# The last feed-forward of a two-layer DiT block: the gate goes into the second weights, the last output slice is made in two halves

## The chip, the cores and the metric

One core of a Trainium2 chip runs the whole program. The metric is the device time of one execution in microseconds (us). Its engines are TensorE (PE, matrix products), VectorE (DVE), ScalarE (ACT), GpSimd (POOL, idle here) and SyncE (SP, which here only issues DMAs). Each engine works through its own queue in order, and waits on semaphores for the others.

## The reference, cut to what matters

The change lies in the last step of the last layer, the second feed-forward (SwiGLU with a gate, 22 blocks of 128 hidden channels), and in the final norm behind it:

```python
# last layer; x is (256 tokens, 1024); m = the layer's nine modulation vectors
h = modulate(rms_norm(x), m[6], m[7])
g, u = jnp.split(h @ w_gu, 2, axis=-1)            # w_gu (1024, 2 * 2816)
x = x + 0.5 * m[8] * ((silu(g) * u) @ w_down)     # w_down (2816, 1024)
return rms_norm(x) * final_gain
```

## The kernel before

All products are in 32-bit pieces: a weight block arrives as a raw 128x2048 tile (`raw`, three buffers), and each of its two halves (128x1024) is split by `Feeder.split` into a high part, which ACT casts (L189), and a low part, raw minus high, which DVE subtracts (L167). A product is then high*high + high*low + low*high. A raw tile is free for the next DMA when both halves are split. At most eight split halves are alive (`feed.limit = 8`).

Which instruction stands where in a queue is decided at build time: `Sched` keeps a clock of estimated PE time, `S.pe(ns)` advances it, and at each step `Feeder.tick` may emit the next split and waiting tasks may emit their next piece. On the chip the queues then run in that fixed order.

`ffn_last` works on pairs of hidden blocks, j = 0, 2, ... 20. For a pair PE makes four projections (g of both blocks, u of both blocks; L1416 and L1420, 24 matmuls each), each into one of four PSUM banks (`ps`) that the pairs reuse in turn. ACT copies one half of the bank (L1432) and DVE adds the other half (L1434), which frees the bank; for g, ACT then makes the silu (L1440); for u, DVE multiplies it in (L1445), ACT casts the result to its high part (L1447) and DVE subtracts the low part (L1450). After the projections of pair j, PE makes the second product (`down`, L1470 to L1472) for the two blocks of pair j - 2, into four other banks `acc[T, h]` (T: tokens 0 to 127 or 128 to 255, h: left or right 512 output columns). In a pair's stretch ACT and DVE therefore also split six halves: four of g and u, and two of the second weights (`f11d...`). The second weights of pair j stand in the plan behind g and u of pair j + 2; those of blocks 20 and 21 (`d10`) stand last.

The last pair's second products are made by `last_down` (L1590 to L1592), one slice (T, h) after the other: first blocks 18 and 19 (`early`), then 20 and 21 (`late`). `residual` then multiplies the slice by the gate (L1549, `grow` is the gate vector spread over all partitions), adds it to the tokens `xtok` (L1550) and ACT squares and sums it (L1553); `root`, `inverse` and `scaled` make the norm, and `store` writes the four slices out, three issued from SP and the last from ACT (L1572).

Ahead of all this, while the norm of x is computed, PE transposes the left half of x to token order (`turn(0, T)`, L1479) and spreads the gate (`spread`, L1487); the right half is transposed after the projections of pair 0 (`turn(1, T)`).

Of the kernel before, what the change touches and what calls it, by code (L numbers as in the profile page):

```python
# [126 lines left out]
class Feeder:  # L127


    def __init__(self, nc, pool, S, tile_):  # L130
        self.nc, self.pool, self.S, self.tile = nc, pool, S, tile_
        self.limit = 6
        self.max_block = 1
        self.next = 0.0
        self.hold = True
        self.lag = 0
        self.part = None
        self.t_dma = {}
        self.plan = []
        self.blocks = []  # L140
        self.index = {}
        self.raw = {}
        self.live = {}
        self.n_dma = self.n_split = 0
        self.raw_live = self.half_live = 0
# [29 lines left out]
    def split(self):  # L175
        self.flush()
        self.load()
        if self.n_split >= len(self.plan) or self.half_live >= self.limit:
            return False
        name, h = self.plan[self.n_split]  # L180
        if name not in self.raw:
            return False
        b = self.blocks[self.index[name]]
        src = b["halves"][h](self.raw[name])
        i = self.n_split
        view = (lambda t: t.rearrange("p (a b) -> p a b", a=src.shape[1])) if len(src.shape) == 3 else (lambda t: t[:, :])
# [68 lines left out]
def tile_hybrid_dit(  # L255
# [86 lines left out]
    def ffn_plan(l, w):  # L342
        gu = (f1_gu, f2_gu)[w][l].rearrange("(k p) c -> p k c", p=P)
        dn = (f1_dn, f2_dn)[w][l].rearrange("(f p) c -> p f c", p=P)
        key = f"f{l}{w}"

        def batch(a, b):
            for f in range(a, b, 2):
                feed.add_block(
                    f"{key}d{f // 2}", [(lambda t: k3(t, 2), dn[:, f:f + 2, :])], None,  # L350
                    [lambda t, h=h: t[:, h * 1024:(h + 1) * 1024] for h in range(2)],
                )
                feed.plan.extend([(f"{key}d{f // 2}", 0), (f"{key}d{f // 2}", 1)])

        alone = l == 1 and w == 1
        for j in range(NF):
            if j % 2 == 0:
                cols_block(f"{key}g{j // 2}", gu[:, :, j * P:(j + 2) * P])
                cols_block(f"{key}u{j // 2}", gu[:, :, DFF + j * P:DFF + (j + 2) * P])
                feed.plan.extend([(f"{key}{nm}{j // 2}", h) for nm in "gu" for h in range(2)])  # L360
                if alone and j:
                    batch(j - 2, j)
            if j in BATCH_AT and not alone:
                batch(*BATCH_AT[j])
        if alone:
            batch(20, 22)
            return
        batch(16, 18)
        batch(18, 22)
# [1037 lines left out]
    def ffn_last(h_task):  # L1407


        key = "f11"  # L1410
        grow, gain, xtok = a4(), a4(), [a4() for _ in range(2)]
        nc.scalar.dma_start(out=gain, in_=final_gain.rearrange("(o p) -> o p", o=1).partition_broadcast(P))
        acts = {}

# [60 lines left out]
        def turn(h, T, copy):  # L1475

            ps = psum()
            for q in range(4):
                nc.tensor.transpose(ps[:, q * P:(q + 1) * P], xT[:, 4 * h + q, T * P:(T + 1) * P], ident)  # L1479
            S.pe(4 * 117)  # L1480
            copy(xtok[T][:, h * 512:(h + 1) * 512], ps)

        def spread(h):

# [8 lines left out]
        wts = [feed.get(k) for k in kk[:3]]  # L1493
        need_ada(1, 8)
        for T in range(2):
            turn(0, T, nc.vector.tensor_copy)
        S.step(h_task)
        spread(0)()
        S.step(h_task)
        owed = spread(1)  # L1500
        wts.append(feed.get(kk[3]))
        S.finish(h_task)
        owed()
        feed.hold = False
        pss = [psum() for _ in kk]
        for k in range(KD):
# [4 lines left out]
        for k in kk:  # L1511
            feed.done(k)
        evict(0, pss)
        for T in range(2):
            turn(1, T, nc.scalar.copy)
        feed.limit = 8
        acc = {}
        order = [(T, h) for T in range(2) for h in range(2)]
# [22 lines left out]
        ss = st(4)  # L1541

        def residual(T, h, parts=1):
            t = t2()
            w = 512 // parts
            for i in range(parts):
                cs = slice(h * 512 + i * w, h * 512 + (i + 1) * w)
                tc_ = t[:, i * w:(i + 1) * w]
                nc.vector.tensor_mul(tc_, acc[T, h][:, i * w:(i + 1) * w], grow[:, cs])  # L1549
                nc.vector.tensor_add(xtok[T][:, cs], xtok[T][:, cs], tc_)  # L1550
            cs = slice(h * 512, (h + 1) * 512)
            i = 2 * T + h
            nc.scalar.activation(out=t2(), in_=xtok[T][:, cs], func=AF.Square, accum_out=ss[:, i:i + 1])  # L1553
            if h == 0:
                nc.scalar.activation(
                    out=ss[:, i:i + 1], in_=ss[:, i:i + 1], func=AF.Identity, bias=epsb[:, 0:1], scale=1.0 / D
                )

        def root(T):
            rms = st(1)  # L1560
            nc.scalar.activation(
                out=rms, in_=ss[:, 2 * T + 1:2 * T + 2], func=AF.Sqrt, bias=ss[:, 2 * T:2 * T + 1], scale=1.0 / D
            )
            return rms

# [3 lines left out]
            return rs  # L1569

        def store(T, h, o):
            (nc.scalar if T and h else nc.sync).dma_start(out=out[T * P:(T + 1) * P, h * 512:(h + 1) * 512], in_=o)  # L1572

        def scaled(T, h, rs):
            cs = slice(h * 512, (h + 1) * 512)
# [3 lines left out]
            )  # L1579
            store(T, h, o)  # L1580

        def last_down(T, h, fs):
            for f in fs:
                if f in act_tasks:
                    S.finish(act_tasks.pop(f))
                whi, wlo = feed.get((f"{key}d{f // 2}", f % 2))
                at = acts[f]
                cs, o = slice(h * 512, (h + 1) * 512), acc[T, h]
                ph, pl = at[:, T * P:(T + 1) * P], at[:, 256 + T * P:256 + (T + 1) * P]
                mm(o, ph, whi[:, cs], start=False, stop=False)  # L1590
                mm(o, pl, whi[:, cs], start=False, stop=False)
                mm(o, ph, wlo[:, cs], start=False, stop=(f == NF - 1))  # L1592
                S.pe(681)

        last_down(0, 0, early)
        last_down(0, 1, early)
        last_down(1, 0, early)
        last_down(0, 0, late)
        residual(0, 0)
        last_down(0, 1, late)  # L1600
        residual(0, 1)
        rms0 = root(0)
        last_down(1, 0, late)
        residual(1, 0)
        rs0 = inverse(rms0)
        scaled(0, 0, rs0)
        last_down(1, 1, early)
        last_down(1, 1, late)
        residual(1, 1, 2)
        xg = t2()  # L1610
        nc.vector.tensor_mul(xg, xtok[1][:, 512:1024], gain[:, 512:1024])
        scaled(0, 1, rs0)
        rs1 = inverse(root(1))
        o = t2()
        nc.scalar.activation(out=o, in_=xg, func=AF.Copy, scale=rs1[:, 0:1])
        scaled(1, 0, rs1)
# [34 lines left out]
```

## Time and profile before

| what | value |
|---|---|
| median of three runs | 1600.36 us (1599.35 to 1601.63) |
| the profiled execution | 1599.29 us, its span 1597.5 us |
| PE busy | 1575.7 us, 99% of the span |
| DVE busy | 1076.9 us, 67% |
| ACT busy | 601.4 us, 38% |
| the last feed-forward | its first projection starts at 1405.04 us, its last matmul at 1588.58 us |

The span is what the trace covers; the execution is 1.8 us longer. Times in rows of the trace are microseconds from the span's start. "Idle before" is the time that the engine stood still ahead of an instruction, with what released it.

### The profile page before, as it was taken

The page shows a single profiled execution, that of the slowest core. Times are in us where ns is not written, and L with a number is a line of the kernel's source. Part 1 is how long each engine was busy: PE and PEld are TensorE (multiplying, and loading weights), DVE is VectorE, ACT ScalarE, POOL GpSimd, SP SyncE. Part 2 cuts the span into 40 slices and gives each one's busy share as a digit, 9 for nine tenths or more (in the row PEclk, how much of TensorE's full clock was granted, in tenths as well). Part 3 has the DMA queues.
Part 4 walks back from the last instruction along what each step waited for, and adds up shares of the span by engine and source line. Part 5 has one row for each costly group of instructions (what it writes and reads, how often), then busy time and mean ns, then how long its engine had stood idle before and what let it go on. Part 6 is the DMA issues. An engine that isn't in the chain of part 4 may idle for free.

```text
span 1597.5 us, 20934 instructions
## 1 busy us (share of the span) xinstructions
PE 1575.7 (99%) x8455; PEld 1320.2 (83%) x8455; DVE 1076.9 (67%) x1672; ACT 601.4 (38%) x1007; POOL 0.8 (0%) x6
## 2 busy tenths in 40 slices
PE   7999999999999999999999999999999999999997
PEld 5888888888886998888888898888888898888886
DVE  4877878786856576765734576766566488776655
ACT  4423231133557452223231343222222356765553
POOL 0000000000000000000000000000000000000000
PEclk9999999999999999999999999999999999999999
DMA  9755565553012434534333315455564224346560
GB/s 333 271 182 198 163 205 200 171 196 106 33 54 54 132 110 164 172 132 158 121 103 106 123 60 184 165 195 184 187 215 165 93 99 101 112 159 223 185 211 27
DMA packets 149345, 241.71 MB, mean 151 GB/s; under 512 B 6484, under 2 KB 115712, under 8 KB 148992
## 3 DMA queue, kind: packets, MB, share of 16 engines
q1 hardware_dynamic: 147008, 238.71, 44.9%
q10 hardware_dynamic: 2240, 1.65, 0.3%
q8 instruction: 67, 1.10, 0.3%
q14 instruction: 30, 0.25, 0.1%
HBM read 239.29 MB, written 1.05 MB: 150 GB/s over the span
## 4 chain that ended last, share of the span: by engine, by line
PE 96%; DVE 2%; SPq 1%; DMA 1%; ACT 0%; issue 0%; ACTq 0%
PE ps L428 24%; PE ps L429 24%; PE ps L430 24%; PE ps L1416 5%; PE ps L1420 3%; PE ps L969 2%; PE ps L971 2%; PE ps L970 2%; PE ps L1190 1%; PE ps L1167 1%; PE ps L1470 1%; PE ps L1472 1%; PE ps L1471 1%; PE ps L654 1%; SPq L328 1%; DMA a<-in_ada_w_dram 1%
## 5 line engine op out<-in xcount | busy, mean ns | idle before, releaser
L428 PE MATMUL ps<-ahi,a 128*128 128x512 f32 (+1 forms) x1312 | 479.6, 366 | 1.2 <-ACT ahi L530 0.7
L429 PE MATMUL ps<-alo,a 128*128 128x512 f32 (+1 forms) x1312 | 477.5, 364 | 0.9 <-DVE alo L534 0.7
L430 PE MATMUL ps<-ahi,a 128*128 128x512 f32 (+1 forms) x1312 | 476.8, 363 | 0.0
L167 DVE TENSOR_TENSOR a<-raw,a 128x1024 fp32r<-128x1024 f32 x296 | 356.4, 1220 | 152.7 <-ACT a L189 152.7
L189 ACT CAST a<-raw 128x1024 fp32r<-128x1024 f32 x296 | 300.4, 1044 | 204.5 <-PE ps L429 78.1
L428 PEld LDWEIGHTS ps<-ahi,a 128*128 128x128 f32 x1312 | 247.4, 189 | 48.2 <-issue 6.0
L429 PEld LDWEIGHTS ps<-alo,a 128*128 128x128 f32 x1312 | 247.5, 189 | 40.4 <-DVE alo L534 1.8
L430 PEld LDWEIGHTS ps<-ahi,a 128*128 128x128 f32 x1312 | 247.4, 189 | 39.3 <-DVE a L212 0.2
L630 DVE SCALAR_TENSOR_TENSOR a<-ada,c,a 128x1024 f32<-128x1024 f32 x196 | 248.8, 1277 | 17.2 <-DMA ada<-in_ada_w_dram 17.1
L428 PE MATMUL ps<-a,a 128*128 128x512 f32 (+1 forms) x624 | 223.8, 359 | 0.0
L430 PE MATMUL ps<-a,a 128*128 128x512 f32 (+1 forms) x624 | 222.5, 357 | 0.0
L429 PE MATMUL ps<-a,a 128*128 128x512 f32 (+1 forms) x624 | 222.4, 356 | 0.0
L763 DVE SCALAR_TENSOR_TENSOR xT<-ps,modT,xT 128x256 f32<-128x256 f32 x288 | 126.5, 477 | 80.5 <-PE ps L430 80.3
L728 ACT CAST a<-t 128x512 fp32r<-128x512 f32 x66 | 41.0, 622 | 253.7 <-DVE t L726 253.7
L428 PEld LDWEIGHTS ps<-a,a 128*128 128x128 f32 x624 | 117.9, 189 | 20.8 <-issue 4.2
L430 PEld LDWEIGHTS ps<-a,a 128*128 128x128 f32 x624 | 117.9, 189 | 17.0
L429 PEld LDWEIGHTS ps<-a,a 128*128 128x128 f32 x624 | 117.9, 189 | 16.7
L721 ACT ACTIVATE t<-ps 128x512 f32<-128x512 f32 x66 | 39.3, 598 | 231.5 <-PE ps L430 225.1
L726 DVE TENSOR_TENSOR t<-ps,t 128x512 f32<-128x512 f32 x66 | 45.3, 690 | 82.1 <-PE ps L430 74.5
L1416 PE MATMUL ps<-ahi,a 128*128 128x512 f32 x352 | 90.5, 392 | 0.7 <-DVE ahi L534 0.7
L1416 PEld LDWEIGHTS ps<-ahi,a 128*128 128x128 f32 x352 | 63.6, 189 | 12.0 <-DVE ahi L534 0.9
L530 ACT ACTIVATE ahi<-t,modT 128x256 fp32r<-128x256 f32 x88 | 43.7, 508 | 54.6 <-DVE t L527 54.5
(176 smaller groups left out, 1378.1 us busy)
## 6 DMA issues: line engine op xcount, KB each, us to landing
raw<-in_ffn_w_gu_dram SPq DMA_DIRECT2D x88, 1024.0 KB, 5.2
ada<-in_ada_w_dram SPq DMA_DIRECT2D x128, 512.0 KB, 5.4
raw<-in_ffn_w_down_dram SPq DMA_DIRECT2D x44, 1024.0 KB, 4.9
raw<-in_w_in_dram SPq DMA_DIRECT2D x10, 1024.0 KB, 5.1
a<-in_ada_w_dram SPq DMA_DIRECT2D x16, 512.0 KB, 8.9
raw<-in_w_out_dram SPq DMA_DIRECT2D x16, 256.0 KB, 4.2
raw<-in_w_out_dram SPq DMA_DIRECT2D x8, 512.0 KB, 6.0
raw<-tab_pool SPq DMA_DIRECT2D x2, 1024.0 KB, 4.8
```

The costliest lines, as they stand in the source:

```text
L167: self.nc.vector.tensor_sub(vl, src, vh.bitcast(F32))
L189: self.nc.scalar.copy(vh, src)
L428: mm(ps, whi, mhi, start=start, stop=False)
L429: mm(ps, whi, mlo, start=False, stop=False)
L430: mm(ps, wlo, mhi, start=False, stop=stop)
L530: nc.scalar.activation(out=ahi[:, d, seg_cols(s)], in_=t, func=AF.Identity, bias=mod(l, m, d, s))
L630: nc.vector.scalar_tensor_tensor(out=acc, in0=raw, scalar=sc, in1=acc, op0=ALU.mult, op1=ALU.add,)
L726: nc.vector.tensor_mul(a[:, :n], u[:, :n], sg[:, :n])
L728: nc.scalar.copy(at[:, 0:n], a[:, :n])
L763: nc.vector.scalar_tensor_tensor(out=xs, in0=ps[:, q * 256:(q + 1) * 256], scalar=mod(l, m0 + 2, d, s), in1=xs, op0=ALU.mult, op1=ALU.add,)
L1416: mm(ps, wt[0][:, k, :], ahi[:, k, :], start=(k == 0), stop=(k == KD - 1))
L1420: mm(ps[:, 0:256], wt[1][:, k, :], ahi[:, k, 0:256], start=False, stop=False)
```

## The change

Three things change, all in the last feed-forward.

1. The gate is multiplied into the second weights. `Feeder.split` now multiplies a half of a `f11d` block by `grow`, in place, on DVE, ahead of ACT's cast of it; in return `residual` no longer multiplies the slice, and adds it straight from PSUM. There are 22 such halves.
2. The last slice (T = 1, right columns) of `last_down` with blocks 20 and 21 is made in two halves of 256 columns, each with its own residual and square, so there are five squares; `scaled(0, 1)` moves ahead of that, and all four stores are issued from SP.
3. `turn(1, T)`, which transposes the right half of x, moves into the norm's wait, ahead of the first projections; its two copies on ACT come right after the norm.

```diff
         src = b["halves"][h](self.raw[name])
+        if name in self.gated:
+            self.nc.vector.tensor_mul(src, src, self.gate)
...
         self.nc.scalar.copy(vh, src)
...
         if alone:
             batch(20, 22)
+            feed.gated.update(f"{key}d{f}" for f in range(NF // 2))
             return
...
+        feed.gate = grow
...
-        owed = spread(1)
+        owed = [spread(1)] + [turn(1, T, nc.scalar.copy) for T in range(2)]
         wts.append(feed.get(kk[3]))
         S.finish(h_task)
-        owed()
+        for late_copy in owed:
+            late_copy()
...
         evict(0, pss)
-        for T in range(2):
-            turn(1, T, nc.scalar.copy)
...
+        def residual(T, c0, c1, i):
+            h, a = divmod(c0, 512)
+            nc.vector.tensor_add(xtok[T][:, c0:c1], xtok[T][:, c0:c1], acc[T, h][:, a:a + c1 - c0])
+            square(T, c0, c1, i)
...
-            (nc.scalar if T and h else nc.sync).dma_start(out=out[T * P:(T + 1) * P, h * 512:(h + 1) * 512], in_=o)
+            nc.sync.dma_start(out=out[T * P:(T + 1) * P, h * 512:(h + 1) * 512], in_=o)
...
         scaled(0, 0, rs0)
-        last_down(1, 1, early)
-        last_down(1, 1, late)
-        residual(1, 1, 2)
+        last_down(1, early, 512, 1024)
+        scaled(0, 1, rs0)
+        last_down(1, late, 512, 768)
+        residual(1, 512, 768, 3)
+        last_down(1, late, 768, 1024)
+        residual(1, 768, 1024, 4)
+        rms1 = root(4)
         xg = t2()
         nc.vector.tensor_mul(xg, xtok[1][:, 512:1024], gain[:, 512:1024])
-        scaled(0, 1, rs0)
-        rs1 = inverse(root(1))
+        rs1 = inverse(rms1)
```

Lines of the kernel shift by a few: the add of a projection is L1434 before and L1440 in the change, the product L1445 and L1451, the low part of an activation L1450 and L1456, the low part of a weight L167 and L169; the new multiply is L188.

DVE's queue in one pair of the kernel before, from the third projection's add to the last split of the pair (`a` and `raw` are split and raw weights, `t` the activations, `ps` a projection's bank; what an instruction waits for stands in brackets):

```order
L1434 TENSOR_TENSOR t_2135_13059<-ps_13034,t_2134_13057 128x256 [waits DVE_49,Activation_49]
L1445 TENSOR_TENSOR t_2135_13059<-t_2135_13059,t_2124_13005 128x256 [waits DVE_49]
L1450 TENSOR_TENSOR t_2136_13062<-t_2135_13059,t_2136_13062 128x256 [waits Activation_49]
L167 TENSOR_TENSOR a_2139_13067<-raw_12957,a_2138_13066 128x1024 [waits DMAHW0_49,Activation_49]
L1434 TENSOR_TENSOR t_2141_13088<-ps_13064,t_2140_13086 128x256 [waits Activation_49]
L1445 TENSOR_TENSOR t_2141_13088<-t_2141_13088,t_2130_13032 128x256 [waits DVE_49]
L1450 TENSOR_TENSOR t_2142_13091<-t_2141_13088,t_2142_13091 128x256 [waits Activation_49]
L167 TENSOR_TENSOR a_2144_13097<-raw_12957,a_2143_13096 128x1024 [waits Activation_49]
```

The same place of DVE's queue in the changed kernel:

```order
L1440 TENSOR_TENSOR t_2135_13075<-ps_13050,t_2134_13073 128x256 [waits DVE_49,Activation_49]
L1451 TENSOR_TENSOR t_2135_13075<-t_2135_13075,t_2124_13021 128x256 [waits DVE_49]
L188 TENSOR_TENSOR raw_12973<-raw_12973,a_1867_11709 128x1024 [waits DMAHW0_49]
L1456 TENSOR_TENSOR t_2136_13078<-t_2135_13075,t_2136_13078 128x256 [waits Activation_49]
L169 TENSOR_TENSOR a_2139_13084<-raw_12973,a_2138_13083 128x1024 [waits Activation_49]
L1440 TENSOR_TENSOR t_2141_13105<-ps_13080,t_2140_13103 128x256 [waits Activation_49]
L1451 TENSOR_TENSOR t_2141_13105<-t_2141_13105,t_2130_13048 128x256 [waits DVE_49]
L188 TENSOR_TENSOR raw_12973<-raw_12973,a_1867_11709 128x1024
L1456 TENSOR_TENSOR t_2142_13108<-t_2141_13105,t_2142_13108 128x256 [waits Activation_49]
L169 TENSOR_TENSOR a_2144_13115<-raw_12973,a_2143_13114 128x1024 [waits Activation_49]
```

Each product is now followed by a multiply of a raw half by the gate (`a_1867`), and ACT's cast of that half, whose result the L169 two rows on takes, waits for it.

DVE's queue where the second weights of blocks 20 and 21 (`raw_13158`) are split, up to the product of block 20, in the changed kernel (in the kernel before the same rows stand there without the two L188):

```order
L169 TENSOR_TENSOR a_2172_13265<-raw_13125,a_2171_13264 128x1024 [waits Activation_49]
L188 TENSOR_TENSOR raw_13158<-raw_13158,a_1867_11709 128x1024 [waits DMAHW4_49]
L169 TENSOR_TENSOR a_2174_13283<-raw_13158,a_2173_13282 128x1024 [waits Activation_49]
L188 TENSOR_TENSOR raw_13158<-raw_13158,a_1867_11709 128x1024
L169 TENSOR_TENSOR a_2177_13299<-raw_13158,a_2176_13298 128x1024 [waits PE_49,Activation_49]
L1440 TENSOR_TENSOR t_2179_13319<-ps_13295,t_2178_13317 128x256 [waits Activation_49]
L1440 TENSOR_TENSOR t_2183_13342<-ps_13323,t_2182_13340 128x256 [waits Activation_49]
L1440 TENSOR_TENSOR t_2187_13365<-ps_13346,t_2186_13363 128x256 [waits DVE_49,Activation_49]
L1451 TENSOR_TENSOR t_2187_13365<-t_2187_13365,t_2180_13321 128x256 [waits DVE_49]
```

All adds of the last pair's projections (L1440) stand behind both multiplies and both subtractions of the last weight block, and so do, on ACT, their copies behind its casts.

PE's queue at the last slice, blocks 20 and 21, in the kernel before (`ps_12042` is `acc[1, 1]`):

```order
L1590 MATMUL ps_12042<-a_2173_13261,t_2188_13346 128x512
L1591 MATMUL ps_12042<-a_2173_13261,t_2188_13346 128x512
L1592 MATMUL ps_12042<-a_2174_13262,t_2188_13346 128x512
L1590 MATMUL ps_12042<-a_2176_13276,t_2192_13371 128x512
L1591 MATMUL ps_12042<-a_2176_13276,t_2192_13371 128x512
L1592 MATMUL ps_12042<-a_2177_13277,t_2192_13371 128x512
```

The same place of PE's queue in the changed kernel (`a_2173` to `a_2177` are the split second weights, `ps_12045` is `acc[1, 1]`):

```order
L1596 MATMUL ps_12045<-a_2173_13282,t_2188_13368 128x256
L1597 MATMUL ps_12045<-a_2173_13282,t_2188_13368 128x256
L1598 MATMUL ps_12045<-a_2174_13283,t_2188_13368 128x256
L1596 MATMUL ps_12045<-a_2176_13298,t_2192_13393 128x256
L1597 MATMUL ps_12045<-a_2176_13298,t_2192_13393 128x256
L1598 MATMUL ps_12045<-a_2177_13299,t_2192_13393 128x256
L1596 MATMUL ps_12045<-a_2173_13282,t_2188_13368 128x256 [waits DVE_49]
L1597 MATMUL ps_12045<-a_2173_13282,t_2188_13368 128x256
L1598 MATMUL ps_12045<-a_2174_13283,t_2188_13368 128x256
L1596 MATMUL ps_12045<-a_2176_13298,t_2192_13393 128x256
```

Six matmuls of 512 columns became twelve of 256, and the seventh waits for DVE: for the add that reads the first half out of the same bank.

## Rows read from the trace of the kernel before

**Rows 1.** The waits of PE, 1395 to 1600 us: us in total, times, longest

```profile
PE ps L1416 <- DVE ahi L534: 0.7, 1, 0.7
```

**Rows 2.** Timeline of DVE, 1441.5 to 1457 us: start, length, instruction

```profile
1441.75 0.42 DVE L1434 TENSOR_TENSOR t<-ps,t 128x256 f32<-128x256 f32 x1
...
1451.15 0.42 DVE L1434 TENSOR_TENSOR t<-ps,t 128x256 f32<-128x256 f32 x1
1451.60 0.42 DVE L1445 TENSOR_TENSOR t<-t,t 128x256 f32<-128x256 f32 x1
...
1453.45 3.50 DVE L167 TENSOR_TENSOR a<-raw,a 128x1024 fp32r<-128x1024 f32 x3 [0.53 <-ACT a L189]
1456.87 0.42 DVE L1434 TENSOR_TENSOR t<-ps,t 128x256 f32<-128x256 f32 x1
```

**Rows 3.** Timeline of ACT, 1441 to 1457 us

```profile
1442.20 0.42 ACT L1440 ACTIVATE t<-t 128x256 f32<-128x256 f32 x1 [1.74 <-DVE t L1434]
...
1452.06 0.41 ACT L1447 CAST t<-t 128x256 fp32r<-128x256 f32 x1 [1.81 <-DVE t L1445]
1452.37 2.94 ACT L189 CAST a<-raw 128x1024 fp32r<-128x1024 f32 x3
1455.22 0.36 ACT L1432 COPY t<-ps 128x256 f32<-128x256 f32 x1
```

**Rows 4.** Timeline of PE: a projection's end, two in a row, the first last_down

```profile
1428.15 0.40 PE L1416 MATMUL ps<-ahi,a 128*128 128x512 f32 x1
...
1572.09 2.00 PE L1416 MATMUL ps<-ahi,a 128*128 128x512 f32 x8
...
1574.88 0.40 PE L1416 MATMUL ps<-ahi,a 128*128 128x512 f32 x1
...
1577.91 0.40 PE L1590 MATMUL ps<-a,t 128*128 128x512 f32 x1
```

**Rows 5.** Groups by line, DVE, 1400 to 1600 us: busy, mean ns, idle before

```profile
L167 DVE TENSOR_TENSOR a<-raw,a 128x1024 fp32r<-128x1024 f32 x62 | 74.1, 1222 | 35.6 <-ACT a L189 35.6
```

**Rows 6.** Timeline of ACT: the copy of pair 2's fourth projection

```profile
1434.76 0.36 ACT L1432 COPY t<-ps 128x256 f32<-128x256 f32 x1
```

**Rows 7.** Timeline: low part of block 21's activation, and its first use on PE

```profile
1579.92 0.43 DVE L1450 TENSOR_TENSOR t<-t,t 128x256 fp32r<-128x256 f32 x1 [0.47 <-ACT t L1447]
...
1582.91 0.39 PE L1591 MATMUL ps<-a,t 128*128 128x512 f32 x1
```

**Rows 8.** Timeline of PE at the first projection and at the right half's transposes

```profile
1405.04 0.50 PE L1416 MATMUL ps<-ahi,a 128*128 128x512 f32 x1 [0.74 <-DVE ahi L534]
...
1416.34 1.03 PE L1479 MATMUL ps<-small,xT 128*128 128x128 f32 x8
1417.13 0.47 PE L1416 MATMUL ps<-ahi,a 128*128 128x512 f32 x1
```

**Rows 9.** Timeline of the end, 1588 to 1594 us

```profile
1588.58 0.39 PE L1592 MATMUL ps<-a,t 128*128 128x512 f32 x1
...
1590.72 0.63 ACT L1553 ACTIVATE t<-a 128x512 f32<-128x512 f32 x1 [1.93 <-DVE a L1550]
...
1591.99 0.16 DVE L1568 RECIPROCAL st<-st 128x1 f32<-128x1 f32 x1
...
1592.24 0.72 ACT L1615 ACTIVATE t<-t,st 128x512 f32<-128x512 f32 x1 [0.47 <-DVE st L1568]
1593.00 0.37 ACTq L1572 DMA_DIRECT2D out_dram<-t  x1
```

**Rows 10.** DMA issues, 1587 to 1598 us: count, KB each, us to landing

```profile
out_dram<-t SPq DMA_DIRECT2D x3, 256.0 KB, 2.0
out_dram<-t ACTq DMA_DIRECT2D x1, 256.0 KB, 3.7
```

**Rows 11.** A stretch behind the last matmul: us, engines' busy time, PEclk, DMA

```profile
1594.00:1595.00 1.00, 0.00 (x0) 0.00 (x0) 0.00 (x0) 0.00 (x0) 0.00 (x0) 0.50 1.00 373
```

**Rows 12.** Timeline of PE: the first transposes of the program

```profile
6.04 3.68 PE L465 MATMUL ps<-small,a 128*128 128x128 f32 x16 [0.94 <-DMA a<-in_x_dram]
```

More of the change, by code (lines that the diff above doesn't have):

```diff
@@ L138, in __init__ @@
         self.t_dma = {}
+        self.gated = set()
+        self.gate = None
         self.plan = []
@@ L1480, in turn @@
             S.pe(4 * 117)
-            copy(xtok[T][:, h * 512:(h + 1) * 512], ps)
+            return lambda: copy(xtok[T][:, h * 512:(h + 1) * 512], ps)
         def spread(h):
@@ L1495, in ffn_last @@
         for T in range(2):
-            turn(0, T, nc.vector.tensor_copy)
+            turn(0, T, nc.vector.tensor_copy)()
         S.step(h_task)
@@ L1540, in ffn_last, with square, root @@
         early, late = range(NF - 4, NF - 2), range(NF - 2, NF)
[L1541 to L1554, printed above, removed]
+        ss = st(5)
+        def square(T, c0, c1, i):
+            nc.scalar.activation(out=t2(F32, 512)[:, 0:c1 - c0], in_=xtok[T][:, c0:c1], func=AF.Square,
+                                 accum_out=ss[:, i:i + 1])
+            if c1 < D:
+                bias = epsb[:, 0:1] if c0 == 0 else ss[:, i - 1:i]
                 nc.scalar.activation(
-                    out=ss[:, i:i + 1], in_=ss[:, i:i + 1], func=AF.Identity, bias=epsb[:, 0:1], scale=1.0 / D
+                    out=ss[:, i:i + 1], in_=ss[:, i:i + 1], func=AF.Identity, bias=bias, scale=1.0 / D
                 )
-        def root(T):
+        def residual(T, c0, c1, i):
+            h, a = divmod(c0, 512)
+            nc.vector.tensor_add(xtok[T][:, c0:c1], xtok[T][:, c0:c1], acc[T, h][:, a:a + c1 - c0])
+            square(T, c0, c1, i)
+        def root(i):
             rms = st(1)
             nc.scalar.activation(
-                out=rms, in_=ss[:, 2 * T + 1:2 * T + 2], func=AF.Sqrt, bias=ss[:, 2 * T:2 * T + 1], scale=1.0 / D
+                out=rms, in_=ss[:, i:i + 1], func=AF.Sqrt, bias=ss[:, i - 1:i], scale=1.0 / D
             )
@@ L1580, in scaled, with last_down @@
             store(T, h, o)
-        def last_down(T, h, fs):
+        def last_down(T, fs, c0, c1):
             for f in fs:
@@ L1587, in last_down @@
                 at = acts[f]
-                cs, o = slice(h * 512, (h + 1) * 512), acc[T, h]
+                h, a = divmod(c0, 512)
+                skip = a > 0
+                cs, o = slice(c0, c1), acc[T, h][:, a:a + c1 - c0]
                 ph, pl = at[:, T * P:(T + 1) * P], at[:, 256 + T * P:256 + (T + 1) * P]
[L1590 to L1604, printed above, removed]
+                mm(o, ph, whi[:, cs], start=False, stop=False, skip_group_check=skip)
+                mm(o, pl, whi[:, cs], start=False, stop=False, skip_group_check=skip)
+                mm(o, ph, wlo[:, cs], start=False, stop=(f == NF - 1), skip_group_check=skip)
+                S.pe(681 if c1 - c0 == 512 else 360)
+        last_down(0, early, 0, 512)
+        last_down(0, early, 512, 1024)
+        last_down(1, early, 0, 512)
+        last_down(0, late, 0, 512)
+        residual(0, 0, 512, 0)
+        last_down(0, late, 512, 1024)
+        residual(0, 512, 1024, 1)
+        rms0 = root(1)
+        last_down(1, late, 0, 512)
+        residual(1, 0, 512, 2)
         rs0 = inverse(rms0)
         scaled(0, 0, rs0)
-        last_down(1, 1, early)
-        last_down(1, 1, late)
-        residual(1, 1, 2)
+        last_down(1, early, 512, 1024)
[5 more added lines that the diff above has]
+        rms1 = root(4)
         xg = t2()
         nc.vector.tensor_mul(xg, xtok[1][:, 512:1024], gain[:, 512:1024])
-        scaled(0, 1, rs0)
-        rs1 = inverse(root(1))
+        rs1 = inverse(rms1)
         o = t2()
```

## The prediction

> **What bounds the kernel now.** I first read who makes PE wait in the last feed-forward: one wait of 0.7 us, for the norm, and none later [rows 1]. So PE's rate sets the time there. A projection takes 2.79 us (1572.09 to 1574.88 in [rows 4], from one last matmul to the next), a matmul of 512 columns 0.227 us (47 steps from 1577.91 to 1588.58, [rows 4, 9]). A pair takes PE 4 x 2.79 + 24 x 0.227 = 16.61 us.
>
> Then I read DVE and ACT where they are late, since there they show how fast they can go by themselves. The copy of pair 2's fourth projection starts at 1434.76 [rows 6], though PE finished it at 1428.15 + 0.40 = 1428.55 [rows 4]: the two engines lag by 6.2 us. While they lag, they need 15.12 us for a pair (first add to first add, 1441.75 to 1456.87, [rows 2]). That is a chain, not a sum of busy time: cast on ACT, subtract on DVE, copy on ACT, add on DVE. DVE stands still 35.6 us ahead of its subtractions, waiting for casts [rows 5]. So the lag shrinks by 1.49 us a pair and is gone near the middle. Both numbers matter: DVE has idle time, but ACT and DVE together have only 1.49 us a pair to spare.
>
> **The gate in the weights.** What it removes: 2.1 us of L1549 in the last 10 us, taken up below. What it adds: 22 multiplies of 128x1024. No such multiply is in the trace; the nearest row is the subtraction of the same shape and engine, 1.22 us [rows 5]. The links of the chain are: add to product 0.45, product to activation's cast 0.46, weight cast to subtraction 1.08, a subtraction and the next DVE row 1.14 (3.42 for three), a weight cast and the next ACT row 0.95 (2.85 for three), add to silu 0.45, ACT's cast of 256 columns and its next row 0.31 [rows 2, 3]. A DVE row overlaps the next by 0.08, so the multiply starts 0.34 behind the product.
>
> Before, product to subtraction of the second weight takes 1.85 us (1451.60 to 1453.45, [rows 2]). In the change the cast waits for the multiply: 0.34 + 1.22 + 0.04 + 1.08 = 2.68, thus 0.83 more, twice a pair. The chain becomes 15.12 + 1.66 = 16.78 us against PE's 16.61. The lag no longer shrinks: it grows by 0.17 a pair. Bounds for a multiply's price: 0, if it all fell into DVE's idle time, and 1.26, if it lay in the chain whole; the waits written in the queues (multiply behind the product, cast behind the multiply) give 0.83.
>
> The lag at the start grows too. Three multiplies stand ahead of pair 2's last copy (two of block pair 0's second weights, one of the next), and four casts that were spread around it now stand ahead of it. With the links above the copy comes at about 1439.2; PE is 0.8 us earlier (below), so the lag is about 11.5 us; 9.5 if only three times 0.83 were added.
>
> A lag has a limit: the next pair's fourth projection needs the bank. It starts 16.61 - 2.79 = 13.82 after the end of this one, and the copy needs 0.13 + 1.14 + 0.42 + 0.05 = 1.74 until the add behind it is done: 12.1 us. From 11.5 it is reached after three to four pairs; then PE waits 0.17 for each pair. Over nine pairs 9 x 0.17 - 0.6 = 0.9, with the wait for the first bank rounded to **+1.1** (0 to 8.2: at 1.26 a multiply the chain is 17.64 and PE waits 1.03 for each of eight pairs).
>
> The bill comes at the end. Let A be the start of the add that frees the bank for pair 20's fourth projection. PE starts it at A + 0.47, ends it at A + 3.26, makes 18 early matmuls and wants block 20's activation at A + 7.35. On the other side stand a product, multiply, cast and subtraction, then the same without product twice for `d10`, and only then the four copies of pair 20: product A + 0.45, multiply 0.79, cast 2.05, subtraction 3.13; multiply 4.27, cast 5.53, subtraction 6.61; multiply 7.75, cast 9.01; copy 9.96, add 11.23, silu 11.68, copy 11.99, add 12.39, silu 12.84, copy 13.15, add 13.55, product 14.00, cast 14.46 to 14.87. PE waits 14.92 - 7.35 = 7.57. Block 20's low part comes 0.45 behind the high one (0.23 of waiting), block 21's high part at A + 16.6, 0.79 late, its low part 0.23 late again. Together **+8.8**. Before, the last low part was 2.56 us early (1579.92 + 0.43 against 1582.91, [rows 7]), because ACT had cast the last weights before pair 20's projections were done.
>
> A wait of 7.6 us touches the clock. Behind the last matmul the granted clock is down to 0.50, which is 1.2 of 2.4 GHz [rows 11]; so I expect that level when PE resumes. The price from a row: at the start of the program 16 transposes take 3.68 us, 0.23 each, where the later eight take 1.03 with 0.11 each [rows 8, 12], about 1.9 us of excess. Part of it falls into the waits for blocks 20 and 21, which are there anyhow: **+0.8** (0 to 1.9). The Trainium skill, "TensorE: Matmul & The Clock Gate", Part 1, says the same of an idle engine: it falls to 1.2 GHz and is released again by activity; by its 426.7 ns for 512 columns at 1.2 GHz, an estimate for the 14 matmuls of the two waits' end would be some 3 us more, of which the waits hide half.
>
> **The last slice in halves.** The six matmuls of the second half wait for the add of the first, whose bank they share. That add comes 0.32 us behind the first half's last matmul (0.28 us for 256 columns and 0.04), `scaled(0, 1)` ahead of it on DVE costs 0.1 more, and it takes 0.42. So PE stands 0.71, and twelve narrow matmuls cost 0.06 more than six wide ones: **+0.77** (0.06 if the wait were not there). On the Trainium skill's page "PSUM — Partial Sum Buffer", section "PSUM bank collisions raise a hardware error", two engines may not touch one bank at once whatever the columns; no row of before shows two such accesses. By a rule on columns alone the 0.71 would be free, by this one it is not, and the queue has the wait.
>
> Behind the last matmul s the chain gets shorter. Before: ACT's final multiply starts at 1592.24, s + 3.66 [rows 9]. Now: end s + 0.28, add s + 0.32 to s + 0.74, square s + 0.78; square to reciprocal was 1.27 (1590.72 to 1591.99, [rows 9]), less 0.21 for half the columns; reciprocal s + 1.84, final multiply s + 2.09. **-1.57**.
>
> The stores: before, the last one starts at 1593.00 from ACT, 0.04 behind that multiply, and lands 3.7 later [rows 9, 10], s + 8.12, beside two others. Now `scaled(1, 0)` ends at s + 2.78, SP issues its store and 0.37 later the last one, s + 3.17; only two are in flight, as the first two left 4 us earlier. The three from SP took 2.0 [rows 10]; with one ahead I take 2.3: s + 5.47. That is 2.65 less than before, 1.57 of it counted: **-1.08** (-1.4 at 2.0; +0.3 at 3.7).
>
> **The transposes.** PE's idle 0.74 us ahead of the first projection is about as long as the eight transposes and what they hold up (1416.34 to 1417.13, [rows 8]), and x is complete by then: **-0.79** (0 if the wait grew by as much). Their two copies on ACT delay the casts by 1.2 us there; in the lag above they are counted, as they leave a place in which they stood a few us later.
>
> **Sum.** -0.79 + 1.1 + 8.8 + 0.8 + 0.77 - 1.57 - 1.08 = +8.0 us on the profiled execution's 1599.29: 1607.3. The runs' median is 1.07 higher, and the forecast goes by it: 1608.4 us.
>
> **The rivals.**
> 1. *The multiplies are hidden (not slower).* DVE is busy 67% of the time and idles ahead of its casts, so they might cost the chain little. Then waits and clock go: -0.79 + 0.77 - 1.57 - 1.08 = -2.7, 1597.7. The end's wait of 7.6 shrinks about as the lag does, so the lag must fall from 11.5 to 4.5 in nine pairs, 0.78 a pair: chain 15.83, a multiply at most 0.36 in place of 0.83. Against it: the cast cannot start before the multiply, nor the multiply before the product.
> 2. *The multiplies cost the chain all of 1.26.* Chain 17.64: 7.1 more on the pairs and 1.3 at the end, 1616.8. For it: a hand-over that I don't see; against: the multiply overlaps the activation's cast.
> 3. *The lag does not reach its limit.* It starts at 9.5 and grows little: 2.5 off the end's wait and no waits in the pairs, 1604.8.
>
> **Numbers.** Forecast 0.80, rival 1 0.08, rival 2 0.07, rival 3 0.05. About 0.2% (3.2 us) is what a measurement can tell here. Slower: forecast, rivals 2 and 3, with a little taken off for the lower ends, 0.90; same 0.08 (rival 1 is 0.17% faster); faster 0.02. The range leaves out rivals 1 and 2 (0.15) and goes by the bounds of clock, stores and lag: 1603.5 to 1613; the forecast's own range is 1604.5 to 1612.
>
> **What would show it.** PE's waits: one of 7 to 8 us for ACT's cast of block 20's activation ahead of the late matmuls, then three below 1 us, and 0.1 to 0.3 us ahead of each later pair's fourth projection. Copies of projections 10 to 12 us behind PE all the way; first adds of pairs 16.8 apart. Granted clock at 0.5 where PE resumes. One wait of 0.7 for the add at the split slice. The last store landing about 5.5 behind the last matmul. Wrong: copies right behind PE's projections in the later pairs (rival 1), or pairs 17.5 apart (rival 2).

## The result, and the profile after

The changed kernel takes 1608.63 us (median of four runs, 1608.50 to 1609.16) where the kernel before takes 1600.13 (1599.35 to 1601.63): 1.0054 times as long, 95% interval 1.004 to 1.0068. The forecast was 1608.4 in a range of 1603.5 to 1613. The profiled execution took 1608.5 us, its span 1606.6; that span is 9.1 longer than the one before, the medians lie 8.5 apart. Points in time below are those of each trace, and the two traces stand 0.18 us apart where the last feed-forward begins.

First who makes PE wait, from 1395 to 1610 us; before, there was the norm's 0.7 alone [rows 1]:

```profile
PE ps L1596 <- ACT t L1453: 7.3, 1, 7.3
PE ps L1596 <- DVE a L1560: 0.6, 1, 0.6
```

The wait for the norm is gone. In its place there is one of 7.3 us for ACT's cast of block 20's activation, and one of 0.6 for the add that reads the split slice's first half.

The cause stands in the timeline of DVE and ACT for one product of pair 18 (start, length, instruction, idle time ahead of it and what ended that):

```profile
1571.13 0.42 DVE L1451 TENSOR_TENSOR t<-t,t 128x256 f32<-128x256 f32 x1
1571.47 1.22 DVE L188 TENSOR_TENSOR raw<-raw,a 128x1024 f32<-128x1024 f32 x1
1571.59 0.41 ACT L1453 CAST t<-t 128x256 fp32r<-128x256 f32 x1 [1.82 <-DVE t L1451]
1572.61 0.42 DVE L1456 TENSOR_TENSOR t<-t,t 128x256 fp32r<-128x256 f32 x1
1572.72 1.06 ACT L193 CAST a<-raw 128x1024 fp32r<-128x1024 f32 x1 [0.73 <-DVE raw L188]
1573.82 1.22 DVE L169 TENSOR_TENSOR a<-raw,a 128x1024 fp32r<-128x1024 f32 x1 [0.79 <-ACT a L193]
```

Product to subtraction takes 2.69 us (1571.13 to 1573.82), 1.85 before [rows 2]. ACT stands 0.73 us ahead of its cast for the multiply, and behind it DVE stands 0.79 for the cast: while either works for the gated half, the other waits.

ACT's copies of the fourth projections show how late the two engines run, here those of pairs 2, 4 and 18:

```profile
1439.39 0.37 ACT L1438 COPY t<-ps 128x256 f32<-128x256 f32 x1
...
1456.17 0.36 ACT L1438 COPY t<-ps 128x256 f32<-128x256 f32 x1
...
1573.68 0.36 ACT L1438 COPY t<-ps 128x256 f32<-128x256 f32 x1
```

The first two are 16.78 us apart, more than PE's 16.61 for a pair; before, 15.12 was possible [rows 2]. PE ended pair 2's fourth projection at 1427.91 (1427.51 and 0.40, next rows), so the lag is 11.48 us; pair 18's copy comes at 1573.68, 11.98 behind PE. By then the lag has come to its limit, the next pair's need of the bank. PE's own waits (L1596 above) don't list it, but those of its weight loads (PEld) do, for the add that frees the bank:

```profile
PEld ps L1422 <- DVE t L1440: 1.4, 6, 0.2
```

That is 0.2 us in each of six pairs.

PE's timeline: the last matmul of pair 2's fourth projection, of pair 18's, then the end:

```profile
1427.51 0.40 PE L1422 MATMUL ps<-ahi,a 128*128 128x512 f32 x1
...
1561.30 0.40 PE L1422 MATMUL ps<-ahi,a 128*128 128x512 f32 x1
...
1578.34 0.40 PE L1596 MATMUL ps<-a,t 128*128 128x512 f32 x1
...
1582.24 0.39 PE L1598 MATMUL ps<-a,t 128*128 128x512 f32 x1
1589.94 0.80 PE L1596 MATMUL ps<-a,t 128*128 128x512 f32 x1 [7.30 <-ACT t L1453]
...
1592.68 0.63 PE L1598 MATMUL ps<-a,t 128*128 128x512 f32 x1
1593.11 0.63 PE L1596 MATMUL ps<-a,t 128*128 128x512 f32 x1
...
1598.21 0.28 PE L1596 MATMUL ps<-a,t 128*128 128x256 f32 x1
...
1598.80 0.28 PE L1598 MATMUL ps<-a,t 128*128 128x256 f32 x1
1599.63 0.39 PE L1596 MATMUL ps<-a,t 128*128 128x256 f32 x1 [0.55 <-DVE a L1560]
...
1600.33 0.28 PE L1598 MATMUL ps<-a,t 128*128 128x256 f32 x1
```

Behind the long wait two matmuls of 512 columns stand 0.43 us apart (1592.68 to 1593.11), not 0.227. The granted clock (the third number from the end of a row) in the wait, behind it, and later says why:

```profile
1583.00:1589.00 6.00, 0.00 (x0) 0.00 (x0) 3.34 (x5) 2.67 (x6) 0.00 (x0) 0.66 0.00 0
1590.00:1595.00 5.00, 4.99 (x11) 3.38 (x12) 2.22 (x5) 2.94 (x7) 0.00 (x0) 0.50 0.01 3
1595.30:1598.00 2.70, 2.70 (x14) 2.19 (x13) 1.61 (x4) 1.26 (x4) 0.00 (x0) 1.00 0.00 0
```

PE stood idle from 1582.6 to 1589.9, came back at half clock, and had the full clock again from about 1595.3.

The end, as ACT's final multiply and the last two stores:

```profile
1602.16 0.72 ACT L1624 ACTIVATE t<-t,st 128x512 f32<-128x512 f32 x1 [0.23 <-DVE st L1572]
...
out_dram<-t SPq DMA_DIRECT2D x2, 256.0 KB, 2.0
```

The multiply starts 1.83 us behind the last matmul's start (3.66 before, [rows 9]), and the span ends 4.44 behind it (5.26 before).

### The profile page after: what moved, and what is told of

Same layout as the page of the kernel before. It is cut to its first block, busy times and chain, and to the rows that moved or that the text cites. A ratio compares the mean times of both kernels' runs of the same rounds, so it can differ in the third digit from the quotient of the medians.

```text
span 1606.6 us, 20969 instructions
## 1 busy us (share of the span) xinstructions
PE 1580.5 (98%) x8461; PEld 1322.9 (82%) x8461; DVE 1097.5 (68%) x1689; ACT 602.1 (37%) x1010; POOL 0.8 (0%) x6
## 4 chain that ended last, share of the span: by engine, by line
PE 85%; DVE 8%; ACT 3%; issue 2%; SPq 1%; DMA 1%; DVEq 0%; ACTq 0%
PE ps L433 24%; PE ps L434 24%; PE ps L435 24%; DVE a L169 3%; ACT a L193 3%; PE ps L974 2%; PE ps L976 2%; PE ps L975 2%; DVE raw L188 2%; PE ps L1195 1%; PE ps L1172 1%; DVE t L1440 1%; PE ps L659 1%; SPq L332 1%; DVE t L1451 1%
## 5 line engine op out<-in xcount | busy, mean ns | idle before, releaser
L169 DVE TENSOR_TENSOR a<-raw,a 128x1024 fp32r<-128x1024 f32 x296 | 357.0, 1222 | 159.0 <-ACT a L193 159.0
```

Source lines behind the costliest of these rows:

```text
L169: self.nc.vector.tensor_sub(vl, src, vh.bitcast(F32))
```

## The experiments

Each kernel ran beside the kernel before on the same chip. Two theories were to be told apart from the forecast's: that the loss comes from the other two parts (*tail*), and that it is DVE's added work, wherever it stands (*work*).

**The gate alone, on the kernel before.** The edit is the multiply in `Feeder.split` and a residual without its own:

```diff
+        if name in self.gated:
+            self.nc.vector.tensor_mul(src, src, self.gate)
...
-                nc.vector.tensor_mul(tc_, acc[T, h][:, i * w:(i + 1) * w], grow[:, cs])
-                nc.vector.tensor_add(xtok[T][:, cs], xtok[T][:, cs], tc_)
+                nc.vector.tensor_add(xtok[T][:, cs], xtok[T][:, cs], acc[T, h][:, i * w:(i + 1) * w])
```

> The kernel before with the first part alone: the gate in the second weights, residual without its multiply; last slice whole, transposes and stores as before. Theory chain (each multiply lengthens the chain of DVE and ACT by 0.83 us, the lag stays, and PE pays at the end): 1600.1 + 1.1 for the pairs + 7.5 for the wait + 2.8 for the half clock and the small waits behind it - 0.8 for the two multiplies that leave the end = 1610.7 us, a wait of PE of 7 to 8 us ahead of the late matmuls, none for a bank. Rival tail (the multiplies are hidden, the loss comes from the split slice and the stores): 1600.1 - 0.8 = 1599.3 us and no wait above 1 us.

It took 1608.48 us (1.0053, 1.004 to 1.0067): nearly the whole loss, with the wait in place, so not *tail*. Waits of PE from 1395 to 1610 us:

```profile
PE ps L1593 <- ACT t L1453: 7.3, 1, 7.3
PE ps L1422 <- DVE ahi L539: 0.7, 1, 0.7
```

It missed the expected 1610.7 by 2.2. The pairs cost 0.1 in place of 1.1, since without the early transposes the lag starts at 10.56 us and grows by 0.17 a pair without coming to its limit before the last pairs; PE's weight loads wait for a bank once, in place of six times:

```profile
PEld ps L1422 <- DVE t L1440: 0.2, 1, 0.2
```

And from the final multiply to the end of the span it takes 4.25 us in place of 5.26 [rows 9, 10], with the last store issued from ACT as before: the first sign that the stores' term had another cause (below, at the last store from ACT).

**The other two parts alone.** The weights are not multiplied, `residual` does it:

```diff
-            feed.gated.update(f"{key}d{f}" for f in range(NF // 2))
...
-            nc.vector.tensor_add(xtok[T][:, c0:c1], xtok[T][:, c0:c1], acc[T, h][:, a:a + c1 - c0])
+            nc.vector.tensor_mul(t, acc[T, h][:, a:a + c1 - c0], grow[:, c0:c1])
+            nc.vector.tensor_add(xtok[T][:, c0:c1], xtok[T][:, c0:c1], t)
```

> The change without its first part: weights not multiplied, residual multiplies each slice by the gate and adds it; halves, order of the end, stores and transposes as in the change. Theory chain: the 1.1 + 7.5 + 2.8 = 11.4 us go, 1608.6 - 11.4 = 1597.2, and the multiplies on DVE give back 0.4 behind the last matmul and up to 0.7 at the bank's wait (DVE also has scaled(0, 0) and scaled(0, 1) ahead of it): 1597.6 to 1598.3 us; PE waits once, 0.7 to 1.5 us, for DVE at the split slice. Rival tail: about 1608 us. Rival work (it is DVE's 22 x 1.14 us of added work that costs, wherever it stands): as chain here.

1598.60 us (0.9993, 0.9984 to 1.0002), 0.3 above the expected stretch; one wait of PE:

```profile
PE ps L1597 <- DVE t L1560: 1.3, 1, 1.3
```

The loss is in the first part. The bank's wait is twice as long here, because `scaled(0, 0)`, `scaled(0, 1)` and two residual multiplies crowd DVE at the end.

**Only the last block gated.** It leaves out the gate of blocks 0 to 19:

```diff
-            feed.gated.update(f"{key}d{f}" for f in range(NF // 2))
+            feed.gated.add(f"{key}d{NF // 2 - 1}")
```

> The change with only the two halves of the last block of second weights (blocks 20 and 21) multiplied by the gate; the other 20 halves stay without it and residual does not multiply, so the output lacks the gate for 20 blocks. Theory chain: without 20 of the multiplies the lag is gone by the middle, and the last two stand before pair 20's projections are done: 1608.6 - 11.4 = 1597.2 us, no wait ahead of the late matmuls. Rival last block (the wait at the end is made by the last two multiplies, which stand ahead of pair 20's copies, and not by a lag that is carried): the wait of 7 us stays, 1606 to 1608 us.

1597.36 us (0.9985, 0.9975 to 0.9994), and of PE's waits only that for the bank is left, so it is the lag that makes the long one. When the lag is gone, the last two multiplies make PE wait for nothing.

**The multiplies one split ahead.** All 22 stay on DVE, and each is issued behind the cast of the split before it (`gate_in` makes a half's multiply unless it has been made):

```diff
         if name in self.gated:
-            self.nc.vector.tensor_mul(src, src, self.gate)
+            self.gate_in(name, h)
...
         self.next = self.S.t + SPLIT_GAP
+        if self.n_split < len(self.plan):
+            name, h = self.plan[self.n_split]
+            if name in self.gated and name in self.raw:
+                self.gate_in(name, h)
         return True
```

> The change with the same 22 multiplies on DVE, each issued one split earlier: behind the cast of the split ahead of it, so that it stands in the time in which DVE waits for that cast (1.42 us ahead of most subtractions, 0.78 ahead of others). The cast of the gated half then finds its data ready. Theory chain: hidden up to some 0.1 us each, the chain of a pair is 15.1 to 15.4 us, under PE's 16.6, the lag drains, and the 1.1 + 7.5 + 2.8 = 11.4 us go: 1597.2 us, PE waits only for the bank of the split slice. Rival work (22 x 1.14 = 25 us more on DVE cost what they cost wherever they stand): 1605 to 1609 us with the wait of 7 us in place.

1597.42 us (0.9985, 0.9977 to 0.9994). DVE does the same work and the loss is gone: *work* has fallen. DVE's timeline around the product of pair 18's first block (its multiply is L182, the subtraction L170, the product L1462):

```profile
1556.64 1.22 DVE L182 TENSOR_TENSOR raw<-raw,a 128x1024 f32<-128x1024 f32 x1
1558.14 1.23 DVE L170 TENSOR_TENSOR a<-raw,a 128x1024 fp32r<-128x1024 f32 x1 [0.29 <-ACT a L200]
1559.29 0.42 DVE L1451 TENSOR_TENSOR t<-ps,t 128x256 f32<-128x256 f32 x1
1559.74 0.43 DVE L1462 TENSOR_TENSOR t<-t,t 128x256 f32<-128x256 f32 x1
1560.08 1.22 DVE L182 TENSOR_TENSOR raw<-raw,a 128x1024 f32<-128x1024 f32 x1
1561.22 0.42 DVE L1467 TENSOR_TENSOR t<-t,t 128x256 fp32r<-128x256 f32 x1
1561.59 1.23 DVE L170 TENSOR_TENSOR a<-raw,a 128x1024 fp32r<-128x1024 f32 x1
```

The multiply takes 1.22 us as in the change, but the wait for the cast ahead of a subtraction is now 0.29 or nothing: it fills the time in which DVE stood still. Product to subtraction is back at 1.85 us (1559.74 to 1561.59).

ACT's copies of the fourth projections of pairs 4 and 6, in the same kernel:

```profile
1452.91 0.37 ACT L1449 COPY t<-ps 128x256 f32<-128x256 f32 x1
...
1468.03 0.37 ACT L1449 COPY t<-ps 128x256 f32<-128x256 f32 x1
```

They are 15.12 us apart, the pace of before (between pairs 2 and 4 it is still 16.78, 1436.13 to 1452.91).

**The wait filled.** On the change, matmuls of zeros, which change no sum, in the long wait:

```diff
+        for _ in range(31):
+            mm(acc[1, 0], nil, whi[:, 0:512], start=False, stop=False)
         last_down(0, late, 0, 512)
```

> The change with 31 matmuls of 512 columns, a stationary tile of zeros against split weights, added into the left bank of tokens 128 to 255 between the early and the late matmuls; they add zeros and stand in the stretch in which PE waits 7.5 us for block 20's activation. They take 31 x 0.227 = 7.0 us. Theory clock (part of the loss is PE's half clock behind the wait): granted clock 1.0 where the late matmuls start; from there to the split slice 24 x 0.227 + 0.23 + 0.78 + 0.23 = 6.7 us in place of 8.27, so 1608.6 - 1.6 = 1607.0 us. Rival waits (the 2.8 us behind the wait are waits for blocks 20 and 21 alone): 1608.6 us, the same.

1607.09 us (1.0043, 1.003 to 1.0057). The granted clock in the wait's place and behind it:

```profile
1583.00:1589.00 6.00, 6.00 (x28) 4.98 (x27) 3.31 (x6) 2.68 (x6) 0.00 (x0) 1.00 0.01 4
1590.00:1595.00 5.00, 4.50 (x18) 3.12 (x18) 2.64 (x6) 3.20 (x7) 0.00 (x0) 1.00 0.00 0
```

From the first late matmul to the split slice it takes 6.83 us (1589.68 to 1596.51) in place of 8.27. So 1.44 us of the change's loss are the clock's: matmuls that compute nothing win 1.5 us by the medians (1.1 when each run is set against the kernel before beside it).

**Another order at the end**, on the run with multiplies one split ahead: the first half of the last slice comes ahead of another bank's late matmuls, so that its add is done when the second half starts:

```diff
+        last_down(1, early, 512, 1024)
+        last_down(1, late, 512, 768)
...
+        residual(1, 512, 768, 2)
         last_down(1, late, 0, 512)
-        residual(1, 0, 512, 2)
+        residual(1, 0, 512, 3)
```

> The run with multiplies one split ahead, and another order at the end: the first half of the last slice comes ahead of the late matmuls of the left columns (tokens 128 to 255), which use another bank, and the second half behind them. Theory bank (PE stands 0.7 us because both halves share a bank and the add reads it): the wait goes, 1597.4 - 0.8 = 1596.6 us, no wait of PE in the last feed-forward. Rival (the wait is covered by the end's chain on DVE, which is as long): 1597.4 us.

1597.13 us (0.9983, 0.9974 to 0.9992), 0.3 less where 0.8 was expected. PE's wait is gone altogether, but ACT's squares of the left columns and of the last half now stand behind each other:

```profile
1589.24 0.63 ACT L1561 ACTIVATE t<-a 128x512 f32<-128x512 f32 x1 [0.42 <-DVE a L1571]
...
1590.19 0.40 ACT L1561 ACTIVATE t<-a 128x256 f32<-128x256 f32 x1
```

This trace is 0.21 us late where the step begins. With that the last matmul starts 0.81 us sooner (1588.72 against 1589.32), as the bank's theory has it, and the final multiply only 0.13 (1591.24 against 1591.16): the wait goes, and most of it had been cover for that chain.

**The last slice whole**, on the run with multiplies one split ahead:

```diff
-        last_down(1, late, 512, 768)
-        residual(1, 512, 768, 3)
-        last_down(1, late, 768, 1024)
-        residual(1, 768, 1024, 4)
+        last_down(1, late, 512, 1024)
+        residual(1, 512, 1024, 3)
```

> The run with multiplies one split ahead, with blocks 20 and 21 of the last slice whole: six matmuls of 512 columns, one add, one square. PE's 0.77 us go; behind the last matmul the chain gets longer: 0.43 + 0.69 + 0.04 to the square, 1.27 to the reciprocal, 0.20 to the multiply = 2.63 us in place of 1.84. Theory even: -0.77 + 0.79, 1597.4 us. If the halves paid as the prediction has it (-1.57 against +0.77): 1598.2 us.

1596.81 us (0.9982, 0.9973 to 0.9991), 0.6 less than with the halves by the medians. Its last matmul and final multiply:

```profile
1588.19 0.39 PE L1609 MATMUL ps<-a,t 128*128 128x512 f32 x1
...
1590.68 0.72 ACT L1633 ACTIVATE t<-t,st 128x512 f32<-128x512 f32 x1 [0.29 <-DVE st L1583]
```

The chain behind the last matmul is 2.49 us, 0.65 longer than with halves (1.84), and the matmul starts 1.13 sooner (0.12 of it the traces' distance): 0.36 less in all. By these traces the halves lose; the medians' 0.6 alone, with intervals that overlap, would not tell.

**The last store from ACT**, on the run with multiplies one split ahead:

```diff
-            nc.sync.dma_start(out=out[T * P:(T + 1) * P, h * 512:(h + 1) * 512], in_=o)
+            (nc.scalar if T and h else nc.sync).dma_start(out=out[T * P:(T + 1) * P, h * 512:(h + 1) * 512], in_=o)
```

> The run with multiplies one split ahead, with the last store issued from ACT as in the kernel before, 0.4 us earlier than SP could. Theory SP (the prediction's term of the stores: from SP the last store lands 1.08 us sooner): 1597.4 + 1.1 = 1598.5 us, 3.7 us from issue to landing. Rival early (the end is shorter since the first two stores are gone when the last ones leave, whichever queue issues them): 1597.0 to 1597.4 us, 2.0 to 2.7 us to landing.

1596.98 us (0.9981, 0.9973 to 0.999), 0.4 less than from SP by the medians; by the traces 4.31 us from the final multiply to the span's end against 4.44. Its stores:

```profile
out_dram<-t SPq DMA_DIRECT2D x3, 256.0 KB, 2.1
out_dram<-t ACTq DMA_DIRECT2D x1, 256.0 KB, 2.7
```

ACT's store lands in 2.7 us, not in the 3.7 of before [rows 10]. So SP as issuer gains nothing. Here the first two stores leave some 4 us ahead of the last ones, where before the second left only 0.9 ahead. A short end does not need that either, for the run with the gate alone issues its stores as the kernel before does. The second and third store from SP in the kernel before (ACT's follows at 1593.00, [rows 9]), then the same and ACT's in the run with the gate alone, and how long that one took to land:

```profile
1592.10 1.20 SPq L1572 DMA_DIRECT2D out_dram<-t  x2
...
1602.51 1.19 SPq L1575 DMA_DIRECT2D out_dram<-t  x2
1603.40 0.37 ACTq L1575 DMA_DIRECT2D out_dram<-t  x1
...
out_dram<-t ACTq DMA_DIRECT2D x1, 256.0 KB, 2.7
```

The second store leaves 0.90 us ahead of ACT's before and 0.89 there, and ACT's lands in 3.7 us before and in 2.7 there. What the trace of the kernel before has at its end, and no other trace here has between its last stores and their landing, is one transfer of 8 KB on a queue that the profile calls instruction (DMA queues of the kernel before, 1592 to 1597.5 us):

```profile
q14 instruction: 1, 0.01, 0.4%
```

Whether it held the last store up, and whether it stands there in every execution, no run shows: what shortened the end is left open.

**The order and ACT's store together.**

> Multiplies one split ahead, the first half of the last slice ahead of the left columns, and the last store issued from ACT: 1597.4 - 0.3 for the order - 0.4 for the store = 1596.7 us, if the two add up; 1597.0 if the store's place covers the order's gain.

1597.47 us (1596.42 to 1598.61; 0.9985, 0.9976 to 0.9994), a wider spread than the others', and above both numbers. By the traces the last feed-forward, from its first transpose to the span's end, takes 194.98 us, and 195.23 in the run with multiplies one split ahead, 195.12 with the order alone, 195.08 with the store alone, 194.85 with the whole slice. So these edits are worth 0.1 to 0.4 us each, and in these traces the rest of the difference comes from ahead of the step; which of them adds to which is left open.

**The multiplies on GpSimd**, which is idle there:

```diff
-            self.nc.vector.tensor_mul(src, src, self.gate)
+            self.nc.gpsimd.tensor_mul(src, src, self.gate)
```

> The change with the 22 multiplies on GpSimd, which has nothing else to do there; a raw tile lands some 20 us before its first cast, so that GpSimd may take up to 8 us for a half. Theory chain: out of the chain of DVE and ACT, the lag drains as without them: 1597.2 us, the lags those of before. Rival contention (GpSimd's work slows DVE or comes too late for the casts): DVE's subtractions above 1.22 us or ACT waiting for GpSimd, and 1600 us or more.

1610.25 us (1.0064, 1.0048 to 1.0079), worse than the change. Groups of DVE and of GpSimd in the last feed-forward (busy us, mean ns):

```profile
L169 DVE TENSOR_TENSOR a<-raw,a 128x1024 fp32r<-128x1024 f32 x62 | 85.0, 1400 | 34.2 <-ACT a L193 34.2
L1451 DVE TENSOR_TENSOR t<-t,t 128x256 f32<-128x256 f32 x22 | 23.3, 1060 | 0.8
L1440 DVE TENSOR_TENSOR t<-ps,t 128x256 f32<-128x256 f32 x44 | 18.4, 417 | 3.7 <-ACT t L1438 3.7
...
L188 POOL TENSOR_TENSOR raw<-raw,a 128x1024 f32<-128x1024 f32 x22 | 63.2, 2896 | 999.3 <-DVE ahi L539 890.9 <-DMA raw<-in_ffn_w_down_dram 91.1 <-DVE t L1440 17.3
```

DVE is rid of the multiplies, and its other instructions take longer: the subtractions 85.0 us in place of 74.1 [rows 5], the products 23.3 in place of 9.4 in the change, the activations' low parts 12.7 in place of 9.1. That is 28.4 us, more than the 26.8 that the multiplies took in the change, and so much of it falls into the chain that PE waits 7.1 us at the banks. GpSimd's own slowness is little of it: ACT's casts wait for it once, 1.9 us.

**The transposes back in their old place**, once in the change and once in the run with multiplies one split ahead:

```diff
-        owed = [spread(1)] + [turn(1, T, nc.scalar.copy) for T in range(2)]
+        owed = [spread(1)]
...
         evict(0, pss)
+        for T in range(2):
+            turn(1, T, nc.scalar.copy)()
```

> The change with the transposes of the right half back behind the projections of pair 0, as in the kernel before; all else as in the change. Prediction's sum: its -0.79 is lost, 1608.6 + 0.8 = 1609.4 us. Rival pace (DVE and ACT pace the whole stretch, so that what PE gains at its start it waits for at the banks): 1608.6 us; PE starts the late matmuls at the same distance from the first projection's start as it did less 0.8, and the pairs' waits are about 0.1 in place of 1.1 us in sum.

> The run with multiplies one split ahead, with the transposes back behind the projections of pair 0. There PE sets the time from the first projection on, so both theories want the full price: 1597.4 + 0.8 = 1598.2 us. If the transposes cost nothing in either place: 1597.4 us.

In the run ahead it took 1598.24 us (0.9991, 0.9983 to 1.0), 0.8 more, as expected. In the change it took 1609.02 us (1608.42 to 1610.15), 0.4 more, between the two numbers (0.9 more when each is set against the kernel before beside it). The trace decides what the medians leave open. ACT's copies of pairs 2 and 4 there:

```profile
1439.57 0.37 ACT L1438 COPY t<-ps 128x256 f32<-128x256 f32 x1
...
1456.35 0.36 ACT L1438 COPY t<-ps 128x256 f32<-128x256 f32 x1
```

The pace is the same 16.78, and the late matmuls start 189.80 us behind the first transpose of the step (1400.27 to 1590.07), 189.93 in the change (1400.01 to 1589.94). So the transposes give the change nothing ahead of the long wait. Its trace is longer only behind the wait, by 0.47 from the first late matmul to the span's end, where PE stays at half clock longer (0.50 in the microsecond from 1595, where the change has 0.91).

## Why the prediction was right, and where its terms were off

**The chain.** Right in each link: the multiply takes 1.22 us (26.8 us for 22), product to subtraction 2.69 (forecast 2.68), a pair 16.78 (16.78), the lag at pair 2 11.48 (11.5), its limit 11.98 (12.1). Rival 1 fell with the gate alone, rival 2 with the pairs' distance (17.64 wanted), rival 3 with the lag at its start.

**Pairs and transposes.** From pair 2's last projection to the end's first matmul it took 1.07 us more (150.83 against 149.76, [rows 4]; forecast 1.1), and the part ahead of it 0.82 less (forecast 0.79). The two terms are right as a sum, but they are not two: in a stretch that DVE and ACT pace, what PE gains at its start it waits for at the banks (six waits in the change, one with the gate alone, which has the transposes in their old place).

**The end's wait.** 7.47 us (1582.24 + 0.23 to 1589.94), forecast 7.57, for ACT's cast of block 20 as named. Its cause is shown by the two runs that take the lag away, with only the last block gated and with the multiplies one split ahead: the wait goes with it.

**The clock.** From 1589.94 to 1598.21 stand 24 matmuls, 5.45 us at 0.227: 2.82 of excess, where 1.25 of waits and 0.8 of clock were forecast. The level was right, 0.50; the price came out too low, for the run with the wait filled shows 1.44, and 1.38 for the waits. It was taken from a row of small transposes at the start of the program, and no view shows half clock there (the windows from 6 to 10 us print 1.00). The prediction's estimate by the Trainium skill, "TensorE: Matmul & The Clock Gate", Part 1, some 3 us of which the waits hide half, was nearer in the net, though it counts 14 matmuls at half clock where the trace has 11 (starts from 1589.94 to 1594.81).

**The split slice.** The bank's wait was there, 0.71 between the starts of the two matmuls beside it less 0.12 (1598.80 to 1599.63), as forecast; with the slower start behind it the term is 0.9 to 1.0 in place of 0.77. Behind the last matmul the chain gained 1.83 (forecast 1.57). But by the run with a whole slice the halves bring only 0.65 of it, less than they cost PE; the other 1.2 (3.66 to 2.49) are there without them, 0.92 already with the gate alone (1599.91 to 1602.65, 2.74), where `residual` has no multiply.

**The stores.** The size was near (0.82, forecast 1.08), but by luck, for neither reason given is borne out: SP as issuer gains nothing, it costs 0.1 to 0.4, and with the gate alone the end is as short (4.25) with the first stores no earlier than before. The forecast took 3.7 us to landing from one execution of the kernel before as the price of its order of stores; the same order lands in 2.7 with the gate alone, and the cause of the difference stays open.

The sum ahead of the last matmul came out 0.9 higher than forecast, most of it the clock. Behind it the two terms together are 2.65, as forecast. With the 0.18 by which the trace was late to begin with that makes 9.1 against 8.0; the medians, which the forecast went by, lie 8.5 apart. So the chain, the lag and the long wait are what the prediction had right; that the sum lies within 0.3 us of the measured 1608.63 is in part luck, for the 0.9 too little and the 0.18 are nearly made up by the 0.7 by which the medians lie closer together than the two profiled executions (1608.50 and 1599.29), and by the 0.2 by which the kernel before ran below the 1600.36 that the forecast added to.

## What to carry to other kernels

An engine's idle time is no room for new work unless the work can stand in it: here the same 22 multiplies on the same engine cost 11 us between a product and the cast that follows it, and nothing that shows one split earlier, where the engine waits for another (1597.42 us with all 22, 1597.36 with the last two alone). Look for the pace of the engines behind PE while they are late, compare it with PE's, and expect the bill at the end of the loop, with the clock's on top. Of the kernels here that compute the whole result, those clearly below the one before (1596.8 to 1597.5 us) keep the gate in the weights, one split ahead, and move the transposes; the lowest median has the last slice whole.

## What the runs showed of the hardware

GpSimd takes 2.90 us for a multiply for which DVE takes 1.22, and while it works DVE's instructions with both operands in SBUF stretch (a product of 0.43 us to 1.06 in the mean), while those with one operand in a PSUM bank stay at 0.42. The Trainium skill, "Advanced Engine Details and Errata", section "GPSIMD Details", says that Pool shares a read and a write interface with DVE, which conflicts with DVE's instructions with two SBUF inputs; the groups agree with it.
